# Split weights kept in DRAM and loaded again, small loads in program order, cache copies in parts: a hybrid attention and SSD layer on one core

## The chip, the cores and the metric

The kernel runs on 1 core of one Trainium2 chip. The metric is device time in microseconds (us). TensorE (PE), VectorE (DVE), ScalarE (ACT) and GpSimd (POOL) compute; SyncE (SP) issues all of the DMAs of this kernel.

## What is computed

One layer of a hybrid decoder on 2048 prompt tokens and 64 sample tokens, width 1024, all in float32:

```
h = rms_norm(x); proj = h @ w_in          # q k v z_a z_s xBC dt g
o_a = window attention (128, 16 heads, sinks, rope on a quarter of a head) * silu(z_a)
o_s = rms_norm(SSD scan of silu(conv(xBC)) * silu(z_s))
y   = x + (sigmoid(g_a) * (o_a @ w_attn_proj) + sigmoid(g_s) * (o_s @ w_ssd_proj)) @ w_out
```

It returns y of both groups, the last 128 keys and values (for the sample group: the caches, moved up by 8 rows, with the new rows behind), the conv rows and the SSM states.

## The kernel before, in words

The prompt is cut into four blocks (0 to 3) of 512 tokens. Three phases each run over the four blocks: T1 (attention's projections and the attention), S (the projections of the SSD branch, conv, and the scan in chunks of 128), and T2 (output projections). The sample tokens ride along in block 2 of T1 and block 0 of S.

A float32 product is made of three products of rounded parts: weights and activations are split into a high part and the rest (`SPLIT3`, L36). A weight tile has 256 columns of w_in by 1024 rows. `wload` (L161) loads it raw (1 MB, L157, pool `wraw` with 2 buffers); `split` (L149) then copies it on ACT to the high part (L150) and subtracts that on DVE (L151); both parts stand in `whl`, 2 MB, of which a phase has two buffers. So the tile after next can be filled only when PE has left a buffer. T1 has 10 tiles in a block, in the order za0, za1, k, v (with 32 more columns for dt), q0, q1, q2, q3, za2, za3; S has in each block 4 groups of 5: bc, x0, x1, z0, z1. Every block loads and splits the same weights again.

PE's projections are L171 (za tiles), L195 (k, v, q tiles, 96 matmuls each) and L184 (S and T2; a tile of S in blocks 1 to 3 has 48 matmuls of 512 columns). Attention units (L522 scores, L539 transposes, L551 products with the values) of one pair of heads run between the tiles that follow; each ends in a DMA of its result, `oa_d` (L563). At the end of a block `load_h` (L315) loads the next block's `hT` in 8 DMAs of 512 KB. In S the scan of group g (`ssd_group`) runs between the projections of group g+1; it ends in a sum of squares on PE (L907), whose row goes through DRAM three times: `ss_d` (L910), `sr` (L914, then the power on POOL), `rs_d` (L917).

`init3` (L227) loads small constants: conv rows, 16 sinks for the sample, `A_log`, `dt_bias`, and `Dcol` (L246: two loads of 64x16 single floats, every second float of D_skip). It is called when block 3 of T1 begins. The copy of the two caches to the output (L643) stands in the sample's attention, behind S.

What runs when on an engine is decided by a scheduler that simulates the program as it is built and may move an instruction ahead of others that it doesn't depend on. All DMAs go through SP's one queue in the order so made: a DMA that has to wait holds up those behind it.

Of the kernel before, what the change touches and what calls it, by code (L numbers as in the profile page):

```python
# [9 lines left out]
F32 = mybir.dt.float32  # L10
F32R = mybir.dt.float32r
# [17 lines left out]
OFF_X = 4608  # L29
# [49 lines left out]
def build(tc, nc, a, o, seq, phases=("T1", "S", "T2"), dbg=None):  # L79
# [66 lines left out]
    wraw_p = top.enter_context(tc.tile_pool(name="wraw", bufs=2))  # L146
    cur = {}

# [11 lines left out]

    def wload(parts):  # L161
        raw, hl = wtile(parts)
        split(hl[:, 0, :, :256], hl[:, 1, :, :256], raw)
        return raw, hl

    def proj_cm(ps, hl, c0, hT, first=True, last=True):
# [49 lines left out]
    def init2():  # L216
# [159 lines left out]
    def phase_t1():  # L376
        with ExitStack() as es:
# [32 lines left out]
            def za_tile(b, pair, hgp, hT, zs):  # L410
                raw, hl = wtile(za_parts(pair, hgp))
                r5 = raw.rearrange("p k (v h d) -> p k v h d", v=2, h=2)
                for hgl in range(2):
                    ov = [hl[:, i, :, hgl * P : hgl * P + P].rearrange("p k (v d) -> p k v d", v=2) for i in range(2)]
                    split(ov[0], ov[1], r5[:, :, :, hgl, :])
                for hgl in range(2):
# [191 lines left out]
    def phase_sa(oas):  # L608
        with ExitStack() as es:
# [108 lines left out]
    def phase_s():  # L718
        with ExitStack() as es:
# [75 lines left out]
            def proj_group(b, g, hT):  # L795
# [14 lines left out]
                for i in range(2):  # L810
                    c = 512 * g + 256 * i
                    _, hl = wload([(0, w_in[:, OFF_X + c : OFF_X + c + 256])])
                    st = sample_tile(smp)
                    for j in range(2):
                        pcs = prompt_pieces(proj_w(mmp, hl, j * P, hT, smp), st[:, j] if smp else None)
                        conv_tile(pcs, 4 * g + 2 * i + j, xT[:, 2 * i + j])
                    if smp:
                        SY.dma_start(xs_d[:, 4 * g + 2 * i : 4 * g + 2 * i + 2], st)
                for i in range(2):
                    c = 512 * g + 256 * i  # L820
                    _, hl = wload([(0, w_in[:, OFF_ZS + c : OFF_ZS + c + 256])])
                    st = sample_tile(smp)
# [506 lines left out]
```

## Time and profile before

| | before |
|---|---|
| median of 3 runs | 3202.14 us (3200.97 to 3202.41) |
| the profiled execution's own time | 3201.39 us |
| its span, first to last instruction | 3199.6 us |
| mean granted TensorE clock | 0.989 of full speed |
| PE busy | 3085.4 us (96%) |
| PE weight loads | 2649.2 us (83%) |
| DVE, ACT, POOL busy | 2081.5 (65%), 1419.9 (44%), 982.5 us (31%) |
| DMA | 448.88 MB, mean 140 GB/s, share of 16 engines 45.2% |

A busy share is of the whole span. T1 takes about the first 717 us, S until about 1944, T2 the rest. The waits of an engine are put down to what came last by the profile; the timeline gives for each stretch of like instructions its start and length, and in brackets how long the engine idled before it and for whom.

### The profile page before, as it was taken

To read this page: it belongs to the slowest core of one execution; us is meant where nothing else is said; L and a number is where in the kernel's file an instruction comes from. 1 tells how busy PE (TensorE), PEld (TensorE's weight loads), DVE (VectorE), ACT (ScalarE), POOL (GpSimd) and SP (SyncE) were. 2 spreads that over 40 slices of the span, in tenths; PEclk is the share of its full clock that TensorE was granted. 3 is DMA by queue.
4 is the path that set the end of the run, shared out by engine and by line. 5 is a ranking of instruction groups with operands and counts; after the bars stand their busy time and mean duration, and the time that the engine had idled before them with its cause. 6 is when DMAs were issued, how large, how long until landed. Compare 5 with 4: busy or idle time off the path is not lost.

```text
span 3199.6 us, 49248 instructions
## 1 busy us (share of the span) xinstructions
PE 3085.4 (96%) x19038; PEld 2649.2 (83%) x19038; DVE 2081.5 (65%) x3265; ACT 1419.9 (44%) x2786; POOL 982.5 (31%) x905
## 2 busy tenths in 40 slices
PE   6999999998999999999999998999999999999999
PEld 5978787877899877777777776787877799999888
DVE  3877868787777787888878886455555554334433
ACT  3544535455555555555656564333233333222321
POOL 1523232231445555555656664000121100000000
PEclk8999999999999999999999998999999999999999
DMA  6544425333433544444454444445655564345443
GB/s 215 157 141 117 141 76 180 108 107 103 126 121 119 172 130 124 154 148 131 129 167 147 129 141 128 139 131 154 205 181 143 155 206 132 99 132 175 137 107 103
DMA packets 472931, 448.88 MB, mean 140 GB/s; under 512 B 33824, under 2 KB 420664, under 8 KB 472648
## 3 DMA queue, kind: packets, MB, share of 16 engines
q1 hardware_dynamic: 472696, 445.73, 45.2%
q8 instruction: 150, 2.46, 0.3%
q14 instruction: 85, 0.70, 0.1%
HBM read 382.39 MB, written 65.35 MB: 140 GB/s over the span
## 4 chain that ended last, share of the span: by engine, by line
PE 73%; DVE 12%; DMA 5%; POOL 5%; issue 3%; ACT 2%; SPq 0%; POOLq 0%; DVEq 0%; ACTq 0%
PE mm L184 46%; PE mm L195 12%; PE mm L171 5%; DVE acc L760 3%; DVE whl L151 2%; POOL L L857 2%; DMA raw<-in_w_in_dram 2%; PE sc L522 1%; PE tr L551 1%; POOL ws L881 1%; DVE zs L897 1%; PE tr L539 1%; PE st L884 1%; DMA xt<-in_x_prompt_dram 1%; ACT whl L150 1%
## 5 line engine op out<-in xcount | busy, mean ns | idle before, releaser
L184 PE MATMUL mm<-hT,whl 128*128 128x512 f32 (+1 forms) x6720 | 1349.1, 357 | 10.4 <-DMA hT<-h_d 4.1
L184 PEld LDWEIGHTS mm<-hT,whl 128*128 128x128 f32 x6720 | 1119.5, 190 | 181.1 <-issue 12.6
L151 DVE TENSOR_TENSOR whl<-raw,whl 128x2048 fp32r<-128x2048 f32 (+1 forms) x232 | 524.6, 2265 | 280.4 <-ACT whl L150 273.0
L184 PE MATMUL mm<-ot,whl 128*128 128x512 f32 (+1 forms) x2880 | 569.1, 355 | 2.8 <-DVE whl L151 2.5
L184 PEld LDWEIGHTS mm<-ot,whl 128*128 128x128 f32 x2880 | 474.2, 188 | 74.9 <-issue 5.7
L150 ACT CAST whl<-raw 128x2048 fp32r<-128x2048 f32 (+1 forms) x232 | 412.7, 1786 | 263.3 <-PE mm L184 132.5
L195 PE MATMUL mm<-whl,hT 128*128 128x256 f32 (+1 forms) x2304 | 307.8, 289 | 23.7 <-DVE zs L421 17.2
L195 PEld LDWEIGHTS mm<-whl,hT 128*128 128x128 f32 x2304 | 290.7, 192 | 28.2 <-DVE zs L421 17.9
L760 DVE SCALAR_TENSOR_TENSOR acc<-cr,cwb,acc 128x512 f32<-128x512 f32 x288 | 284.5, 990 | 15.8 <-ACT acc L755 7.0
L857 POOL TENSOR_TENSOR L<-L,cbm 128x1024 f32<-128x1024 f32 x64 | 182.5, 2861 | 94.4 <-DVE cbm L846 92.8
L195 PE MATMUL mm<-whl,ot 128*128 128x256 f32 (+1 forms) x1632 | 203.9, 285 | 0.0
L195 PEld LDWEIGHTS mm<-whl,ot 128*128 128x128 f32 (+1 forms) x1632 | 197.6, 188 | 5.3 <-issue 4.9
L171 PE MATMUL mm<-hT,whl 128*128 128x512 f32 x768 | 194.3, 403 | 2.3 <-ACT hT L277 2.1
L855 ACT ACTIVATE L<-AB,acs 128x128 f32<-128x128 f32 x512 | 157.0, 389 | 38.6 <-PE py L878 29.0
L171 PEld LDWEIGHTS mm<-hT,whl 128*128 128x128 f32 x768 | 142.8, 192 | 33.8 <-ACT hT L277 2.5
L368 ACT ACTIVATE s<-s,ng 128x128 f32<-128x128 f32 x256 | 99.9, 393 | 94.4 <-DVE ng L362 84.2
L150 ACT CAST ot<-v 128x512 fp32r<-128x512 f32 x96 | 58.9, 620 | 162.1 <-DVE v L1195 86.9
L881 POOL TENSOR_TENSOR ws<-wx,ws 128x512 fp32r<-128x512 f32 x64 | 112.2, 1752 | 10.1 <-ACT ws L880 9.8
L374 POOL TENSOR_SCALAR s<-s,den 128x128 f32<-128x128 f32 x128 | 50.1, 403 | 202.7 <-DVE den L370 140.6
L826 ACT ACTIVATE th<-mm 128x512 f32<-128x512 f32 (+1 forms) x80 | 40.0, 509 | 160.8 <-PE mm L184 153.6
L764 ACT ACTIVATE th<-acc 128x512 f32<-128x512 f32 x96 | 60.5, 630 | 111.8 <-DVE acc L760 111.7
L1187 ACT ACTIVATE t<-mm 128x512 f32<-128x512 f32 (+1 forms) x76 | 37.6, 518 | 162.4 <-PE mm L184 141.9
(318 smaller groups left out, 3912.5 us busy)
## 6 DMA issues: line engine op xcount, KB each, us to landing
raw<-in_w_in_dram SPq DMA_DIRECT2D x120, 1024.0 KB
hT<-h_d SPq DMA_DIRECT2D x80, 512.0 KB
raw<-in_w_in_dram SPq DMA_DIRECT2D x64, 512.0 KB
AB<-ac_d SPq DMA_DIRECT2D x64, 512.0 KB
raw<-in_w_ssd_proj_dram SPq DMA_DIRECT2D x32, 1024.0 KB
v_d<-zs SPq DMA_DIRECT2D x16, 1024.0 KB
v<-v_d SPq DMA_DIRECT2D x64, 256.0 KB
raw<-in_w_attn_proj_dram SPq DMA_DIRECT2D x64, 256.0 KB
```

The costliest lines, as they stand in the source:

```text
L150: A.copy(hi, src)
L151: V.tensor_tensor(lo, src, hi.bitcast(F32), ALU.subtract)
L171: PE.matmul(ps, hl[:, x, k, c0 : c0 + P], ht[:, y, :], start=first and i == 0, stop=last and i == n - 1,)
L184: PE.matmul(ps, hl[:, x, k, c0 : c0 + P], ht[:, y, lo : lo + n], start=i == 0, stop=i == 3 * len(hT) - 1,)
L195: PE.matmul(ps, ht[:, x, tt * P : tt * P + m], hl[:, y, k, :n], start=i == 0, stop=i == 3 * len(hT) - 1,)
L368: A.activation(s[:, i, :width], s[:, i, :width], AF.Exp, bias=ng[:, i : i + 1], accum_out=den[:, i : i + 1])
L374: G.tensor_scalar(s[:, i, :width], s[:, i, :width], den[:, i : i + 1], 0.5, ALU.mult, ALU.mult)
L760: V.scalar_tensor_tensor(out=acc, in0=raw[:, k : k + TB], scalar=cwb[:, k, ct : ct + 1], in1=acc, op0=ALU.mult, op1=ALU.add)
L764: A.activation(th, acc, AF.Tanh)
L855: A.activation(L[:, h], AB[:, h], AF.Relu, scale=-1.0, bias=acs[:, hc.start + h : hc.start + h + 1])
L857: G.tensor_tensor(L, L, cbm[:, c].unsqueeze(1).to_broadcast([P, 8, P]), ALU.mult)
L881: G.tensor_tensor(ws[:, 1], wx, ws[:, 0].bitcast(F32), ALU.subtract)
```

## The change

Three edits; T2, and the arithmetic, are as before, and PE's instructions are the same in kind and number.

1. `store` writes the split tile `whl` (2 MB) to DRAM when a block has first made it: 10 tiles in T1's block 0 and 20 in S's block 0. `reload` loads such a tile (2 MB) straight to `whl` in blocks 1 and 3 of T1 (20 tiles; block 2 has the sample, which needs the raw tile, and loads and splits as before) and in blocks 1 to 3 of S (60 tiles). These 80 tiles have no raw load, no copy on ACT and no subtraction on DVE.
2. The small loads of `init3` are kept in program order by `late`: they can't be moved ahead of DMAs that stand before them in the program.
3. The copies of the caches, two DMAs of 960 KB, become 16 of 120 KB, a pair behind each second group of S, in program order too.

```diff
-    def wload(parts):
+    def wload(parts, key=None, keep=True):
+        if key in kept:
+            return None, reload(key)
         raw, hl = wtile(parts)
         split(hl[:, 0, :, :256], hl[:, 1, :, :256], raw)
+        if key is not None and keep:
+            store(key, hl)
         return raw, hl
+
+    def store(key, hl, w=256):
+        if key not in kept:
+            kept[key] = dt_("w_d" + "_".join(map(str, key)), [P, 2, KT, w]), w
+            SY.dma_start(kept[key][0], hl[:, :, :, :w].bitcast(F32))
+
+    def reload(key):
+        hl = cur["whl"].tile([P, 2, KT, cur["w"]], F32R, name="whl", tag="whl")
+        src, w = kept[key]
+        SY.dma_start(hl[:, :, :, :w].bitcast(F32), src)
+        return hl
...
+    def late(dst, src):
+        tc.keep_in_program_order(SY.dma_start(dst, src))
...
         for hl in range(2):
-            SY.dma_start(Dcol[64 * hl : 64 * hl + 64], dv[hl].partition_broadcast(64))
+            late(Dcol[64 * hl : 64 * hl + 64], dv[hl].partition_broadcast(64))
...
             def za_tile(b, pair, hgp, hT, zs):
+                key = ("za", pair, hgp)
+                if key in kept and b != sb:
+                    hl = reload(key)
+                else:
...
+                    store(key, hl)
...
-                raw, hl = wload([(0, w_in[:, OFF_K : OFF_K + 256])])
+                raw, hl = wload([(0, w_in[:, OFF_K : OFF_K + 256])], None if b == sb else ("k",))
...
-                SY.dma_start(ow[:, 0:120], a[f"cache_{nm}"][0].rearrange("b j h d -> b j (h d)")[:, 8:P])
...
-                _, hl = wload([(0, w_in[:, cb : cb + P]), (P, w_in[:, cc : cc + P])])
+                _, hl = wload([(0, w_in[:, cb : cb + P]), (P, w_in[:, cc : cc + P])], ("bc", g))
...
                     stats(b, g)
+                    for nm in ("k", "v"):
+                        for r in range((4 * b + g) * 8 // (4 * NB), (4 * b + g + 1) * 8 // (4 * NB)):
+                            late(o[f"{nm}_win_s"][r, 0:120], a[f"cache_{nm}"][0, r, 8:P].rearrange("j h d -> j (h d)"))
```

The other tiles of T1 and S get their keys in the same way. The order of the instructions follows from the scheduler, so it is shown at four places. Lines of the changed kernel are numbered otherwise: there L173 is `store`, L178 `reload`, L243 the loads of `late`; L300 is L282 of before, L308 is L290, L333 is L315, L588 is L563, L876, L886, L922, L934, L938 and L941 are L852, L862, L898, L910, L914 and L917. Names with numbers at their end are tensors in DRAM; 128x1024 of `hT` is 512 KB.

**The start, on SP** (T1's block 0, tiles k and v). Before:

```order
L240 DMA A_bc<-in_A_log_dram 128x32
L282 DMA h_d_1_61<-hT 128x1024
L243 DMA dtb_bc<-in_dt_bias_dram 128x32
L246 DMA Dcol<-in_D_skip_dram 64x16x1 x2
L290 DMA xt<-in_x_prompt_dram 128x1024
L282 DMA h_d_1_61<-hT 128x1024
L290 DMA xt<-in_x_prompt_dram 128x1024
L643 DMA out_dram<-in_cache_k_dram 8x2x15360
L282 DMA h_d_1_61<-hT 128x1024
L643 DMA out_dram<-in_cache_v_dram 8x2x15360
L157 DMA raw<-in_w_in_dram 128x8x256 x3
```

And now:

```order
L173 DMA w_dza_0_332<-whl 2048x1x256
L157 DMA raw<-in_w_in_dram 128x8x256
L300 DMA h_d_0_60<-hT 128x1024 x3
L173 DMA w_dza_1_398<-whl 2048x1x256
L157 DMA raw<-in_w_in_dram 128x8x256
L300 DMA h_d_0_60<-hT 128x1024
L599 DMA tab_2450<-in_rope_p_dram 128x4x80
L300 DMA h_d_1_61<-hT 128x1024 x2
L308 DMA xt<-in_x_prompt_dram 128x1024 x2
L300 DMA h_d_1_61<-hT 128x1024 x2
L173 DMA w_dk<-whl 2048x1x256
L157 DMA raw<-in_w_in_dram 128x8x256
```

The small loads of `init3` are gone from here, `Dcol` among them, and so are the cache copies; the stores of the tiles za0, za1, k and v stand between the others.

**The end of T1's block 0, on SP**, where the next block's `hT` is loaded. Before:

```order
L563 DMA oa_d_0_68<-zs 128x4x128
L157 DMA raw<-in_w_in_dram 128x8x256
L315 DMA hT<-h_d_0_62 128x1024 x4
L563 DMA oa_d_0_68<-zs 128x4x128
L315 DMA hT<-h_d_1_63 128x1024 x4
```

And now:

```order
L588 DMA oa_d_0_68<-zs 128x4x128
L178 DMA whl<-w_dza_1_398 128x16x256
L333 DMA hT<-h_d_0_62 128x1024 x4
L333 DMA hT<-h_d_1_63 128x1024 x3
L588 DMA oa_d_0_68<-zs 128x4x128
```

The reload of za1 for block 1 (`w_dza_1_398`) stands directly ahead of the 8 loads of `hT`; it writes to the buffer that PE's last tile of block 0 (za3) reads. **On PE** this is now the end of block 0 (L186 is L171 of before, L564 and L576 are L539 and L551), the last row being block 1's first tile:

```order
L186 MATMUL mm<-hT,whl 128x512 x2
L576 MATMUL tr<-PT,vT 64x512 x4
L564 MATMUL tr<-cst,s 128x128 x8
L576 MATMUL tr<-PT,vT 64x512 x4
L564 MATMUL tr<-cst,s 128x128 x8
L186 MATMUL mm<-hT,whl 128x512 x12
```

Between the last matmul of za3 and the first of block 1 there are two products with the values and two runs of transposes.

**T1's block 3, on SP**, from the results of block 2's last attention unit on. Before:

```order
L563 DMA oa_d_1_73<-zs 128x4x128
L446 DMA out_dram<-qr 128x256
L475 DMA out_dram<-vT 128x256
L157 DMA raw<-in_w_in_dram 128x8x256
L563 DMA oa_d_1_73<-zs 128x4x128
L473 DMA dt_d_115<-dtt 128x128
L157 DMA raw<-in_w_in_dram 128x8x128 x6
```

And now:

```order
L588 DMA oa_d_1_73<-zs 128x4x128
L243 DMA rows_6516<-in_conv_w_dram 96x128
L243 DMA rows_6516<-in_conv_b_dram 24x128
L243 DMA rows_6516<-in_ssd_norm_w_dram 16x128
L243 DMA sinkS<-in_sinks_dram 8x1 x16
L243 DMA A_bc<-in_A_log_dram 128x32
L243 DMA dtb_bc<-in_dt_bias_dram 128x32
L243 DMA Dcol<-in_D_skip_dram 64x16x1 x2
L498 DMA dt_d_115<-dtt 128x128
L500 DMA out_dram<-vT 128x256
L178 DMA whl<-w_dq_924 128x16x256
L178 DMA whl<-w_dq_1536 128x16x256
```

The small loads now stand here; the reload of q1 (`w_dq_924`) is behind them.

**The end of a group in S, on SP.** Before (a raw bc tile is two loads of 128 columns):

```order
L898 DMA v_d_1_81<-zs 128x4x512
L157 DMA raw<-in_w_in_dram 128x8x128 x2
L157 DMA raw<-in_w_in_dram 128x8x256
L910 DMA ss_d_1_101<-sm 1x512
L914 DMA sr<-ss_d_1_101 128x4
L917 DMA rs_d_1_121<-sr 128x4
L157 DMA raw<-in_w_in_dram 128x8x256 x2
```

And now, with a pair of cache copies:

```order
L922 DMA v_d_1_85<-zs 128x4x512
L886 DMA EB<-ac_d_94 64x4x128
L178 DMA whl<-w_dz_1_10873 128x4096
L934 DMA ss_d_1_105<-sm 1x512
L938 DMA sr<-ss_d_1_105 128x4
L941 DMA rs_d_1_125<-sr 128x4
L243 DMA out_dram<-in_cache_k_dram 16x1920
L243 DMA out_dram<-in_cache_v_dram 16x1920
L178 DMA whl<-w_dbc_11240 128x4096
```

The raw loads of bc and x0 stood ahead of `ss_d` before; now the reload of the next group's bc stands behind `rs_d` and the copies. The same place **on PE** now (L931 is L907 of before, L199 is L184, L862 to L890 are the first steps of the next scan, ahead of the next bc tile):

```order
L199 MATMUL mm<-hT,whl 128x512 x59
L931 MATMUL st<-thl,onesr 32x512
L199 MATMUL mm<-hT,whl 128x512 x5
L931 MATMUL st<-thl,onesr 32x512
L199 MATMUL mm<-hT,whl 128x512 x25
L862 MATMUL tr<-cst,BT 128x128
L199 MATMUL mm<-hT,whl 128x512 x48
L862 MATMUL tr<-cst,BT 128x128 x3
L868 MATMUL tr<-CT,BT 128x128 x4
L890 MATMUL po<-CT,H_8427 128x128 x4
L199 MATMUL mm<-hT,whl 128x512 x19
```

Behind the second L931 there are 25 and 48 matmuls of the tiles z0 and z1 and then 8 short instructions before the first matmul of the next bc tile.

## Rows read from the trace of the kernel before

**Rows 1.** Windows by stage: us, busy of each engine (instructions), PE clock, DMA share, GB/s.

```profile
0.00:200.00 200.00, 165.85 (x1056) 145.35 (x1057) 120.67 (x223) 86.37 (x185) 58.40 (x77) 0.95 0.60 191
200.00:707.00 507.00, 497.07 (x3564) 427.46 (x3564) 389.09 (x838) 242.12 (x718) 155.67 (x215) 0.99 0.37 113
717.00:1066.00 349.00, 333.40 (x2480) 312.36 (x2478) 249.22 (x419) 189.62 (x429) 144.65 (x131) 0.97 0.38 119
1066.00:1944.00 878.00, 850.32 (x4522) 689.00 (x4522) 712.96 (x808) 511.06 (x896) 513.15 (x401) 1.00 0.45 143
```

**Rows 2.** PE's waits, whole span: engine, line, releaser: us, times, longest us.

```profile
PE mm L195 <- DVE zs L421: 17.2, 2, 16.1
...
PE py L878 <- DVE xT L894: 10.2, 9, 1.3
...
PE po L866 <- DVE H L891: 7.7, 13, 1.2
```

**Rows 3.** Timeline at the start, all engines: start us, us, engine, line, operation.

```profile
40.22 0.33 SPq L243 DMA_DIRECT2D dtb_bc<-in_dt_bias_dram  x1
...
40.59 1.44 SPq L246 DMA_DIRECT2D Dcol<-in_D_skip_dram  x2
...
52.29 5.80 SPq L290 DMA_DIRECT2D xt<-in_x_prompt_dram  x1
...
63.94 1.06 ACT L251 ACTIVATE junk<-xt 128x1024 bf16<-128x1024 f32 x1 [20.95 <-DMA xt<-in_x_prompt_dram]
...
66.34 1.01 PE L195 MATMUL mm<-whl,hT 128*128 128x256 f32 x3 [16.10 <-DVE zs L421]
```

**Rows 4.** Windows, columns as in group 1: two stretches of the start, then T1's end.

```profile
42.00:61.00 19.00, 7.13 (x54) 6.34 (x52) 2.33 (x3) 0.23 (x1) 0.00 (x0) 0.85 0.06 7
55.30:72.40 17.10, 6.06 (x28) 6.06 (x29) 6.11 (x6) 5.86 (x9) 1.46 (x4) 0.50 0.62 244
714.00:721.00 7.00, 4.32 (x19) 4.32 (x20) 6.84 (x17) 2.22 (x4) 1.28 (x1) 0.51 1.04 384
```

**Rows 5.** The page's costliest groups: the split of the weights on VectorE and ScalarE.

```profile
L151 DVE TENSOR_TENSOR whl<-raw,whl 128x2048 fp32r<-128x2048 f32 (+1 forms) x232 | 524.6, 2265 | 280.4 <-ACT whl L150 273.0
...
L150 ACT CAST whl<-raw 128x2048 fp32r<-128x2048 f32 (+1 forms) x232 | 412.7, 1786 | 263.3 <-PE mm L184 132.5
```

**Rows 6.** SP's queue, timeline at the end of T1's block 0.

```profile
168.91 2.42 SPq L315 DMA_DIRECT2D hT<-h_d  x4
```

**Rows 7.** PE's timeline in T1's block 3: parts of tiles v and q0.

```profile
600.79 4.76 PE L195 MATMUL mm<-whl,hT 128*128 128x288 f32 x34
...
605.48 1.94 PE L551 MATMUL tr<-PT,vT 128*64 128x512 f32 x8
...
607.76 5.44 PE L195 MATMUL mm<-whl,hT 128*128 128x288 f32 x39
...
620.28 4.75 PE L195 MATMUL mm<-whl,hT 128*128 128x256 f32 x38
```

**Rows 8.** SP's queue, timeline in S, block 1: two group ends.

```profile
1198.12 0.25 SPq L910 DMA_DIRECT2D ss_d<-sm  x1
1200.76 0.35 SPq L914 DMA_DIRECT2D sr<-ss_d  x1
1203.88 0.33 SPq L917 DMA_DIRECT2D rs_d<-sr  x1
...
1266.14 0.39 SPq L910 DMA_DIRECT2D ss_d<-sm  x1
1270.79 0.35 SPq L914 DMA_DIRECT2D sr<-ss_d  x1
1275.67 0.33 SPq L917 DMA_DIRECT2D rs_d<-sr  x1
```

**Rows 9.** PE's timeline in S, block 1, at the second of those group ends.

```profile
1263.89 0.40 PE L907 MATMUL st<-thl,onesr 128*32 128x512 f32 x1
1264.12 16.49 PE L184 MATMUL mm<-hT,whl 128*128 128x512 f32 x72
```

More of the change, by code (lines that the diff above doesn't have):

```diff
@@ L146, in build @@
     wraw_p = top.enter_context(tc.tile_pool(name="wraw", bufs=2))
-    cur = {}
+    cur, kept = {}, {}
     def split(hi, lo, src, **kw):
@@ L225, in init2 @@
         V.tensor_scalar(wrow[:, 0], wrow[:, 0], 0.125, None, ALU.mult)
+    def late(dst, src):
+        tc.keep_in_program_order(SY.dma_start(dst, src))
     def init3(xp, trp):
         rows = xp.tile([P, 2, P], F32, name="rows3", tag="xt")
-        SY.dma_start(rows[:96, 0], a["conv_w"][0].rearrange("k (c p) -> (k c) p", p=P))
-        SY.dma_start(rows[96:120, 0], a["conv_b"][0].rearrange("(c p) -> c p", p=P))
-        SY.dma_start(rows[:16, 1], a["ssd_norm_w"][0].rearrange("(c p) -> c p", p=P))
+        late(rows[:96, 0], a["conv_w"][0].rearrange("k (c p) -> (k c) p", p=P))
+        late(rows[96:120, 0], a["conv_b"][0].rearrange("(c p) -> c p", p=P))
+        late(rows[:16, 1], a["ssd_norm_w"][0].rearrange("(c p) -> c p", p=P))
         ips = trp.tile([P, 256], F32, name="tr", tag="tr")
@@ L237, in init3 @@
         for h in range(NH):
-            SY.dma_start(sinkS[8 * h : 8 * h + 8], a["sinks"][0][h : h + 1].partition_broadcast(8))
+            late(sinkS[8 * h : 8 * h + 8], a["sinks"][0][h : h + 1].partition_broadcast(8))
         V.tensor_scalar(nsinkS, sinkS, -1.0, None, ALU.mult)
-        SY.dma_start(A_bc, a["A_log"][0].partition_broadcast(P))
+        late(A_bc, a["A_log"][0].partition_broadcast(P))
         A.activation(A_bc, A_bc, AF.Exp)
         V.tensor_scalar(A_bc, A_bc, -1.0, None, ALU.mult)
-        SY.dma_start(dtb_bc, a["dt_bias"][0].partition_broadcast(P))
+        late(dtb_bc, a["dt_bias"][0].partition_broadcast(P))
         dv = a["D_skip"][0].rearrange("(c l) -> l c", l=2)
         for hl in range(2):
-            SY.dma_start(Dcol[64 * hl : 64 * hl + 64], dv[hl].partition_broadcast(64))
+            late(Dcol[64 * hl : 64 * hl + 64], dv[hl].partition_broadcast(64))
     def norm_x(xt, jp, nwb, n=P):
@@ L410, in za_tile @@
             def za_tile(b, pair, hgp, hT, zs):
[L411 to L415, printed above, removed]
+                key = ("za", pair, hgp)
+                if key in kept and b != sb:
+                    hl = reload(key)
+                else:
+                    raw, hl = wtile(za_parts(pair, hgp))
+                    r5 = raw.rearrange("p k (v h d) -> p k v h d", v=2, h=2)
+                    for hgl in range(2):
+                        ov = [hl[:, i, :, hgl * P : hgl * P + P].rearrange("p k (v d) -> p k v d", v=2) for i in range(2)]
+                        split(ov[0], ov[1], r5[:, :, :, hgl, :])
+                    store(key, hl)
                 for hgl in range(2):
@@ L462, in v_tile @@
                     SY.dma_start(raw_dt, w_in[:, OFF_DT : OFF_DT + 32].rearrange("(k p) c -> p k c", p=P))
-                raw, hl = wload([(0, w_in[:, OFF_V : OFF_V + 256])])
-                split(hl[:, 0, :, 256:288], hl[:, 1, :, 256:288], raw_dt)
+                raw, hl = wload([(0, w_in[:, OFF_V : OFF_V + 256])], None if b == sb else ("v",), keep=False)
+                if raw is not None:
+                    split(hl[:, 0, :, 256:288], hl[:, 1, :, 256:288], raw_dt)
+                    store(("v",), hl, 288)
                 if b > 0:
@@ L484, in q_tile @@
             def q_tile(b, kv, hT, tab):
-                raw, hl = wload([(0, w_in[:, kv * 256 : kv * 256 + 256])])
+                raw, hl = wload([(0, w_in[:, kv * 256 : kv * 256 + 256])], None if b == sb else ("q", kv))
                 out = []
@@ L811, in proj_group @@
                     c = 512 * g + 256 * i
-                    _, hl = wload([(0, w_in[:, OFF_X + c : OFF_X + c + 256])])
+                    _, hl = wload([(0, w_in[:, OFF_X + c : OFF_X + c + 256])], ("x", g, i))
                     st = sample_tile(smp)
@@ L820, in proj_group @@
                     c = 512 * g + 256 * i
-                    _, hl = wload([(0, w_in[:, OFF_ZS + c : OFF_ZS + c + 256])])
+                    _, hl = wload([(0, w_in[:, OFF_ZS + c : OFF_ZS + c + 256])], ("z", g, i))
                     st = sample_tile(smp)
```

## The prediction

> **What bounds the kernel now.** I read the windows by stage first, since a busy share over the whole span mixes three phases. PE is the engine that is always nearly full: it is idle for 34.2 of the first 200 us, for 9.9 us up to 707 us, for 15.6 us in S's first block and for 27.7 us in the other three blocks of S (length of the stretch less PE's busy time) [rows 1]. DVE is next, at 713.0 of 878 us in S's blocks 1 to 3. So the copies and subtractions that the change takes away, long as they are, sit on engines that have room, and the change is worth what it does to PE's idle time and PE's clock. PE's own waits come second: the largest single one is 16.1 us at a place where DVE makes `zs` [rows 2]; the others are many and about 1 us each, on DVE's `xT` and `H`. Third, the timeline of the start shows where the 16.1 us come from [rows 3]: the two `Dcol` loads are issued at 40.59, the issue of the `xt` load behind them takes 5.80 us, and in 42 to 61 us the DMA engines carry 7 GB/s at a share of 0.06 [rows 4]. Those loads are 2048 pieces of 4 bytes; they block the queue for about 20 us. ACT waits 20.95 us for `xt`, and PE's wait ends when ACT and DVE go on. Afterwards the granted clock is 0.50 until 72.4 us [rows 4], which is the level of 1.2 GHz.
>
> All sums are against the profiled execution, 3201.39 us; the median of the three runs is 0.75 us above that, so what holds for one holds for the other. A difference under 0.2%, 6.4 us, can't be told from none here.
>
> **The start.** The `Dcol` loads leave, and with them the sinks' loads that held up DVE. PE's wait of 17.2 us [rows 2] goes, and the 6.1 us of work at half clock behind it (66.34 to 72.4) [rows 3, 4] takes 3.0 less: -20. What is late next: two stores of 2 MB now stand ahead of the v tile's raw load, and two more follow. At the 384 GB/s that the queue reached at the end of T1 [rows 4], 2 MB is 5.5 us. K's raw load is then some 5.5 us later and v's 11, and both still come while PE is on the tiles before (za1 and k, over 11 us each), so I cost the stores at nothing here; if that cover is gone, see the third rival.
>
> **The end of T1's block 0.** The reload of za1 must wait until PE has left za3, and the 8 `hT` loads are behind it. Before, four of them were issued at 168.91, with PE still on za3 [rows 6]. Now hT's first 512 KB come 5.5 us (2 MB) and 1.4 us later, plus a completion of 1.5 to 3 us (the round trip of a load of 2 KB is 2.6 us from issue to issue) [rows 8], so 8.4 to 10 us after za3. PE has two products of 1.94 us [rows 7] and the transposes between, some 6 us. The stall is 3 to 4 us; a pause of this kind has cost some time at half clock as well. I take +7, from +3 to +10.
>
> **Block 3 of T1.** `Dcol` is still loaded, only later, and the reload of q1 is queued behind it. Counted from the start of v: unit 3's result is at about +12, since its products stand in the middle of v; 21 small loads at 0.33 us [rows 3] put `Dcol` at +19; it drains until +39, by the 20 us of the start; 2 MB more land at +45. PE wants q1 after v (96 matmuls at 139 ns [rows 7]: 13.4 us), q0 (96 at 125 ns: 12.0 us) and transposes: about +30. That is a stall of 15 us, with 3 us of half clock as at the start: +18. Before, nothing of the kind stood there. So the largest stall is moved, not removed.
>
> **S, block 0.** 20 stores of 2 MB in 349 us add 120 GB/s to the 119 there [rows 1]; a store follows the split and its buffer is read by PE for longer than it takes. +3 for queueing, bounds 0 and +10.
>
> **S, blocks 1 to 3.** 60 tiles lose 1.8 us of ACT and 2.27 us of DVE [rows 5], some 245 us of the two engines, none of it on PE's path as such. What it can give back is PE's idle time, 27.7 us [rows 1], which is mostly the short waits for DVE (10.2 us for `xT`, 7.7 us for `H`) [rows 2]. DVE loses 11.4 us in a group of 73 us, so I let half of it go: -14 (nothing at the one end, -25 at the other). Against that stand the reloads. A buffer is free when PE leaves a tile and wanted one tile later, 48 matmuls of 229 ns, 11.0 us [rows 9]; 2 MB need 5.5 us at the 384 GB/s and at most some 10 with a slow round trip, so a reload that is issued at once comes in time. The bc tile of the next group isn't: its reload is behind `ss_d`, `sr`, `rs_d` and two copies. From PE's second L907 it was 2.2 us to `ss_d` [rows 8, 9]; the two steps behind took 2.6 and 3.1 us at the one group end and 4.7 and 4.9 us at the other [rows 8]; with 1.1 us for the copies' issue the reload is issued at +9.0 to +12.9 us and lands between +15 and +22. PE wants it after 73 matmuls, 16.7 us, and 2 us of short work: +18.7. The middle, about 18.5, is just in time. I take half a microsecond late on average over 12 groups: +6, bounds 0 and +40. Sum for these blocks: -8.
>
> The Trainium skill has a rule for this (DMA: Bandwidth & Descriptors, "Anatomy of one DMA": a transfer costs about 2.0 us plus its bytes over 436 GB/s, fitted for DMAs that GpSimd issues). It would give an estimate of 6.8 us for a reload, with the chain as above +15.8 to +19.7; by it the bc tile is late in the worst case only, these blocks give -14, and the total is 6 us lower. I stay with the rows, whose best rate is 384 GB/s.
>
> **The rest.** T1's blocks 1 and 3 lose 20 splits, and their idle time is small (9.9 us in 507) [rows 1]; the cache copies leave the busy start. -5, bounds -10 and 0. T2 is unchanged. **Sum:** -20 + 7 + 18 + 3 - 8 - 5 = -5, so about 3196 us. Its own range is 3180 to 3212, by the bounds above.
>
> **Rivals.**
> 1. *The reloads come late in S, and the kernel is slower.* The place is the bc tile at the 12 group ends; it decides once load and chain exceed 18.7 us. With the slow steps (+12.9) and a 2 MB load of 9 us it is 3.2 us late: 12 x 3.2 = 38, and the -14 shrinks too, since the tiles behind z1 are held by the same queue; 3196 - 6 + 38 = 3228, up to 3240. For it: the queue carries twice the bytes, and the steps of 4.7 us were measured with 2 MB of raw loads in flight. Against: there, three raw loads were ahead of `ss_d`, and now it is one reload, issued 6 us earlier. A sentence of the Trainium skill speaks for it (DMA: Bandwidth & Descriptors, "Latency and other measured facts": access to HBM takes 0.2 us on average and 2 us at high load); the steps of 2.6 and 4.7 us agree with a latency that grows under load. Chance 0.24.
> 2. *`Dcol` in block 3 doesn't reach PE* (it drains faster when nothing else is asked for, or q1's order differs in time): without the +18, 3178. Against it: the 19 us of nearly empty DMA engines [rows 4] had no other traffic in them. Chance 0.17.
> 3. *The stall at the start stays*: stores of 2 MB ahead of the raw loads and of `xt` take the place of `Dcol`. 8 MB at 384 GB/s are 22 us of queue, and if half of that falls on PE, +12, with its clock: 3211. Against it: each load has over 11 us of PE's work as cover. Chance 0.12.
>
> **How the numbers follow.** The forecast has 0.47. Faster by over 0.2% is below 3195.7, slower above 3208.5. The forecast lies at the first bound; of its 0.47 I give 0.25 to faster, 0.17 to the same and 0.05 to slower; the first rival is slower (0.22) or, if only just late, the same (0.02), the second is faster (0.17), the third slower (0.08) or the same (0.04). So faster 0.42, the same 0.23, slower 0.35. The range of 8 in 10 goes from 3168 (the second rival with a little more of S's waits gone) to 3232 (most of the first).
>
> **What would show it.** Right: no wait of 16 us of PE near 50 us; a wait of PE at the start of q1 in block 3 of 10 us or more with the DMA engines nearly empty ahead of it; a few us of waiting for `hT` at the end of block 0; in S's blocks 1 to 3, PE's waits for `xT` and `H` about halved, and a wait for the bc reload of under 1 us per group. Wrong: waits of PE on reloads of several us at each group end (first rival), no wait at q1 (second), a wait near 50 us for k or v (third).

## The result, and the profile after

The changed kernel took 3184.4 us (median of 4 runs, 3183.07 to 3188.17) beside 3202.27 us (4 runs, 3200.97 to 3208.05): a ratio of 0.9943, 95% interval 0.9925 to 0.9960. It is faster, by 0.4 to 0.75%. The profiled execution has a span of 3182.0 us at a mean clock of 0.990, 17.6 us less than before. DMA moved 596.45 MB instead of 448.88.

The 17.6 us are the small remainder of larger amounts of both signs. The table gives the time at which PE begins or ends certain tiles, found by counting the matmuls of its projection lines in the trace (48 or 96 a tile). The lead is after less before; a step is what the lead changed by since the row above.

| mark | before | after | lead | step |
|---|---|---|---|---|
| T1 block 0: q1 begins | 102.5 | 83.6 | -18.9 | -18.9 |
| block 0: za3 ends | 177.6 | 157.8 | -19.8 | -0.9 |
| block 1: za1 ends | 213.9 | 200.3 | -13.6 | +6.2 |
| block 1: q0 begins | 255.4 | 236.6 | -18.8 | -5.2 |
| block 2: first tile begins | 349.7 | 329.6 | -20.1 | -1.3 |
| block 3: q0 ends | 631.8 | 610.3 | -21.6 | -1.5 |
| block 3: q1 begins | 631.7 | 628.3 | -3.4 | +18.2 |
| block 3: za3 ends | 707.2 | 708.8 | +1.5 | +4.9 |
| S: first tile begins | 717.4 | 713.0 | -4.5 | -6.0 |
| S: block 1 begins | 1068.0 | 1066.7 | -1.3 | +3.2 |
| S: last tile ends | 1943.9 | 1929.0 | -14.9 | -13.6 |
| end of the span | 3199.6 | 3182.0 | -17.6 | -2.7 |

The order of PE's attention units differs between the two kernels, so a mark can stand ahead of work that the other kernel has already done. At q1 of block 0 and at block 2's first tile both have done the same (the count in brackets behind PE's busy time is of its matmuls), before and after:

```profile
102.50:349.70 247.20, 240.62 (x1642) 210.78 (x1641) 195.41 (x426) 131.36 (x368) 86.34 (x115) 0.99 0.49 148
```

```profile
83.63:329.60 245.97, 239.30 (x1643) 208.89 (x1642) 181.98 (x419) 114.59 (x353) 83.65 (x118) 0.99 0.75 240
```

Between them the lead grows by 1.3 us, and PE idles for as long as before (6.7 us for 6.6). In the step of +6.2 at za1's end PE does 190 matmuls where it had done 159 (from za3's end on, both with 96 of the projections): attention work that had its place before za3's end or behind za1's. Of the -5.2 behind it 3.6 us are a wait for `dtt` that PE no longer has.

**The start.** PE's timeline after, where 16.10 us of idle time stood [rows 3]:

```profile
43.71 16.51 PE L210 MATMUL mm<-whl,hT 128*128 128x256 f32 x133
```

and ACT's, in the same place:

```profile
43.91 0.60 ACT L443 ACTIVATE th<-mm 128x512 f32<-128x512 f32 x1 [2.34 <-PE mm L186]
...
47.34 1.91 ACT L150 CAST whl<-raw 128x2048 fp32r<-128x2048 f32 x1 [2.54 <-DMA raw<-in_w_in_dram]
...
52.88 1.06 ACT L269 ACTIVATE junk<-xt 128x1024 bf16<-128x1024 f32 x1 [2.66 <-DMA xt<-in_x_prompt_dram]
```

PE goes through k and v without a pause. ACT's tanh comes ahead of its work on `xt`, and that waits 2.66 us for its load instead of 20.95.

**Block 3 of T1.** SP's queue after:

```profile
593.11 5.38 SPq L243 DMA_DIRECT2D sinkS<-in_sinks_dram  x16
...
599.41 1.37 SPq L243 DMA_DIRECT2D Dcol<-in_D_skip_dram  x2
600.88 3.20 SPq L498 DMA_DIRECT2D dt_d<-dtt  x1
604.18 0.74 SPq L500 DMA_DIRECT2D out_dram<-vT  x1
605.01 17.25 SPq L178 DMA_DIRECT2D whl<-w_dq  x2
```

PE's timeline there:

```profile
611.96 0.63 PE L521 MATMUL tr<-cst,qr 128*128 128x128 f32 x4 [1.26 <-DVE qr L369]
628.29 8.31 PE L210 MATMUL mm<-whl,hT 128*128 128x256 f32 x49 [15.70 <-DMA whl<-w_dq]
```

and the windows at that place (columns as in [rows 1]):

```profile
616.30:633.40 17.10, 5.11 (x24) 5.14 (x25) 0.20 (x1) 0.00 (x0) 0.00 (x0) 0.50 0.79 257
```

`Dcol` is issued at 599.41, 18.1 us after v began (k ended at 581.4). The issues of the two reloads behind it end only 17.25 us after the first began; q1's is out by 606.1, but from 604 to 616 us the DMA engines are at a share of 0.05 and carry nothing that counts (0 GB/s). PE waits 15.70 us for q1's reload, and the clock is granted at 0.50, the level of 1.2 GHz, until 633.4.

**The end of block 0.** SP and PE, after:

```profile
158.59 0.78 SPq L178 DMA_DIRECT2D whl<-w_dza  x1
...
160.03 5.53 SPq L333 DMA_DIRECT2D hT<-h_d  x7
...
164.95 2.98 PE L576 MATMUL tr<-PT,vT 128*64 128x512 f32 x8 [3.02 <-DVE PT L566]
...
169.97 3.06 PE L186 MATMUL mm<-hT,whl 128*128 128x512 f32 x12 [0.43 <-DMA hT<-h_d]
```

hT is issued 2.2 us after za3's end at 157.8 and PE starts on it at 169.97. In between PE has only attention units, with waits of 1.13 and 3.02 us for `PT`, DVE's copy of their transposed weights. The last wait is the one for hT (0.43 us): without the waits for `PT`, PE would have waited for hT instead, and block 1 could not have begun much earlier.

**PE's waits over the whole span**, after [rows 2]:

```profile
PE mm L210 <- DMA whl<-w_dq: 15.7, 1, 15.7
...
PE py L902 <- DVE xT L918: 5.1, 5, 1.3
PE po L890 <- DVE H L915: 5.0, 2, 2.6
```

The waits for `xT` are half of the 10.2 us of before, those for `H` 5.0 instead of 7.7. The windows after, S's block 0 and blocks 1 to 3:

```profile
717.00:1066.00 349.00, 329.76 (x2450) 307.41 (x2449) 242.93 (x418) 186.39 (x428) 143.25 (x130) 0.98 0.72 244
...
1066.70:1929.00 862.30, 849.04 (x4509) 688.10 (x4507) 577.14 (x745) 404.51 (x830) 439.79 (x401) 1.00 0.63 218
```

In blocks 1 to 3 PE is idle for 13.3 us (862.30 less 849.04), where it had been 27.7; DVE has 577 us of work instead of 711 in the same stretch of before. In block 0 the stores raise the traffic from 119 to 244 GB/s. The splits that are left, on the page after [rows 5]:

```profile
L151 DVE TENSOR_TENSOR whl<-raw,whl 128x2048 fp32r<-128x2048 f32 (+1 forms) x144 | 319.4, 2221 | 253.9 <-ACT whl L150 248.9
...
L150 ACT CAST whl<-raw 128x2048 fp32r<-128x2048 f32 (+1 forms) x144 | 259.6, 1810 | 239.7 <-PE mm L199 128.2
```

205 us of DVE and 153 us of ACT are gone, and 17.6 us of the span.

**The end of a group in S**, block 1, after, on SP and on PE:

```profile
1251.95 0.32 SPq L178 DMA_DIRECT2D whl<-w_dz  x1
1259.84 0.24 SPq L934 DMA_DIRECT2D ss_d<-sm  x1
1260.97 0.33 SPq L938 DMA_DIRECT2D sr<-ss_d  x1
1264.00 0.32 SPq L941 DMA_DIRECT2D rs_d<-sr  x1
...
1265.69 0.53 SPq L178 DMA_DIRECT2D whl<-w_dbc  x1
```

```profile
1257.22 0.40 PE L931 MATMUL st<-thl,onesr 128*32 128x512 f32 x1
...
1276.17 4.13 PE L199 MATMUL mm<-hT,whl 128*128 128x512 f32 x17
```

From the second L931 to the first matmul of the next bc tile it is 18.95 us; its reload is issued at +8.5 us, and PE doesn't wait for it. The trace has ten group ends whose reload stands behind `rs_d` in this way: it is issued at +7.2 to +13.6 us (median 9.6), and PE begins the tile 9.5 to 12.9 us after the issue, at none of them waiting for the reload. All waits of PE for reloads in blocks 1 to 3 come to 0.7 us.

### The profile page after: what moved, and what is told of

Its sections match the earlier page's. It is cut to its first block, busy times and chain, and to the rows that moved or that the text cites. A ratio compares the mean times of both kernels' runs of the same rounds, so it can differ in the third digit from the quotient of the medians.

```text
span 3182.0 us, 49035 instructions
## 1 busy us (share of the span) xinstructions
PE 3085.6 (97%) x19038; PEld 2647.9 (83%) x19038; DVE 1905.2 (60%) x3175; ACT 1279.3 (40%) x2696; POOL 900.8 (28%) x905
## 2 busy tenths in 40 slices
DMA packets 437073, 596.45 MB, mean 187 GB/s; under 512 B 34224, under 2 KB 373960, under 8 KB 426200
## 4 chain that ended last, share of the span: by engine, by line
PE 76%; DVE 9%; DMA 6%; POOL 4%; issue 3%; ACT 2%; SPq 1%; DVEq 0%; ACTq 0%; POOLq 0%
PE mm L199 50%; PE mm L210 11%; PE mm L186 5%; DVE acc L784 2%; PE tr L576 2%; DMA hT<-h_d 2%; PE sc L547 1%; PE py L902 1%; POOL ws L905 1%; POOL L L881 1%; PE st L908 1%; PE po L890 1%; PE tr L564 1%; DMA whl<-w_dq 1%; DMA h_d<-hst 1%
## 5 line engine op out<-in xcount | busy, mean ns | idle before, releaser
L199 PE MATMUL mm<-hT,whl 128*128 128x512 f32 (+1 forms) x6720 | 1343.6, 356 | 11.5 <-DMA hT<-h_d 6.9
L199 PEld LDWEIGHTS mm<-hT,whl 128*128 128x128 f32 x6720 | 1116.9, 189 | 182.9 <-issue 12.5
L199 PE MATMUL mm<-ot,whl 128*128 128x512 f32 (+1 forms) x2880 | 571.7, 356 | 2.2 <-ACT ot L150 2.2
L199 PEld LDWEIGHTS mm<-ot,whl 128*128 128x128 f32 x2880 | 476.1, 189 | 74.7 <-issue 5.7
L151 DVE TENSOR_TENSOR whl<-raw,whl 128x2048 fp32r<-128x2048 f32 (+1 forms) x144 | 319.4, 2221 | 253.9 <-ACT whl L150 248.9
L150 ACT CAST whl<-raw 128x2048 fp32r<-128x2048 f32 (+1 forms) x144 | 259.6, 1810 | 239.7 <-PE mm L199 128.2
L784 DVE SCALAR_TENSOR_TENSOR acc<-cr,cwb,acc 128x512 f32<-128x512 f32 x288 | 274.2, 953 | 27.2 <-ACT acc L779 24.8
L881 POOL TENSOR_TENSOR L<-L,cbm 128x1024 f32<-128x1024 f32 x64 | 162.2, 2545 | 143.8 <-DVE cbm L870 136.9
L186 PE MATMUL mm<-hT,whl 128*128 128x512 f32 x768 | 192.9, 401 | 3.4 <-ACT hT L295 2.3
L186 PEld LDWEIGHTS mm<-hT,whl 128*128 128x128 f32 x768 | 141.7, 190 | 35.4 <-ACT hT L295 2.7
L851 DVE SCALAR_TENSOR_TENSOR zs<-th,mm 128x512 f32<-128x512 f32 (+1 forms) x80 | 45.7, 578 | 150.0 <-ACT th L850 149.4
L905 POOL TENSOR_TENSOR ws<-wx,ws 128x512 fp32r<-128x512 f32 x64 | 105.8, 1653 | 5.1 <-ACT ws L904 4.9
```

The source lines that it names most:

```text
L150: A.copy(hi, src)
L151: V.tensor_tensor(lo, src, hi.bitcast(F32), ALU.subtract)
L186: PE.matmul(ps, hl[:, x, k, c0 : c0 + P], ht[:, y, :], start=first and i == 0, stop=last and i == n - 1,)
L199: PE.matmul(ps, hl[:, x, k, c0 : c0 + P], ht[:, y, lo : lo + n], start=i == 0, stop=i == 3 * len(hT) - 1,)
L784: V.scalar_tensor_tensor(out=acc, in0=raw[:, k : k + TB], scalar=cwb[:, k, ct : ct + 1], in1=acc, op0=ALU.mult, op1=ALU.add)
L881: G.tensor_tensor(L, L, cbm[:, c].unsqueeze(1).to_broadcast([P, 8, P]), ALU.mult)
```

## The experiments

Each ratio is against runs of the kernel before on the same chip in the same session; the medians of before were 3202.3 to 3205.5 in them, so ratios are compared, and medians only within a few us. Marks are those of the table above.

**1. Reloads without the new order.** The small loads may be moved again, and the cache copies are as before.

```diff
     def late(dst, src):
-        tc.keep_in_program_order(SY.dma_start(dst, src))
+        SY.dma_start(dst, src)
```

> Stores and reloads as in the changed kernel, but the small loads and the cache copies free to be moved, as before. Theory A (the moved loads took the stall from the start, about -19 us, and put it at q1 of block 3, about +18; the reloads are worth about -14 in S's blocks 1 to 3): PE's stall of some 16 us near 50 us is back, no stall at q1, so the two cancel and the time is that of the changed kernel within 6 us, 3184 (3178 to 3190). In the order hT stands ahead of za1's reload, which should take some 5 us off the end of block 0: 3180 is likeliest. Theory B (the whole gain is the moved loads; the reloads give nothing): 3200.

Measured: 3185.17 us, ratio 0.9943 (0.9926 to 0.9959). PE's longest wait, from its waits over the whole span:

```profile
PE mm L210 <- ACT whl L150: 19.3, 1, 19.3
```

SP's queue in that run:

```profile
57.99 0.97 SPq L243 DMA_DIRECT2D Dcol<-in_D_skip_dram  x1
59.01 1.34 SPq L668 DMA_DIRECT2D out_dram<-in_cache_k_dram  x1
60.40 0.68 SPq L668 DMA_DIRECT2D out_dram<-in_cache_v_dram  x1
61.20 5.44 SPq L173 DMA_DIRECT2D w_dk<-whl  x1
66.69 21.11 SPq L157 DMA_DIRECT2D raw<-in_w_in_dram  x1
```

The stall is back at the start, at 78.5 us instead of 50 and 19.3 us long: the two `Dcol` loads were moved to 54 and 58 us, and the raw load behind them takes 21 us to issue. It isn't `Dcol`'s alone: the cache copies (1.9 MB) and the store of k (2 MB) stand between, and from 80 to 82 us, with PE idle, the DMA engines are at a share of 0.91. There is none at q1. With hT ahead of za1's reload the step at the end of block 0 is 1.2 us (lead +7.6 at za3's end, +8.8 at za1's) where it was 6.2, with 182 matmuls in it for 190. So the reloads alone are worth what the change is worth, though the stall of the start stays; theory B falls.

**2. The new order without reloads.** No tile is stored.

```diff
-        if key is not None and keep:
-            store(key, hl)
...
-                    store(key, hl)
...
-                    store(("v",), hl, 288)
```

> The small loads in program order and the cache copies in parts, no stores and no reloads. Theory A: no stall at the start (-19), a stall at block 3 behind Dcol of 10 to 18 us (a raw load of 1 MB and the split behind it instead of 2 MB): 3195 to 3202, about 3199. Theory B (the moved loads are the gain): 3184.

Measured: 3184.15 us, ratio 0.9939 (0.9925 to 0.9954). That is the number of theory B, and a miss for mine: the start is 22.1 us shorter, and no stall comes up at block 3, where the lead at q1 is still -22.8. SP's queue and the windows there:

```profile
598.88 0.39 SPq L157 DMA_DIRECT2D raw<-in_w_in_dram  x1
...
611.64 1.40 SPq L241 DMA_DIRECT2D Dcol<-in_D_skip_dram  x2
```

```profile
611.00:632.00 21.00, 21.00 (x182) 21.00 (x181) 15.64 (x28) 8.63 (x14) 13.86 (x12) 1.00 0.06 4
```

The DMA engines are as empty behind `Dcol` as before (share 0.06, 4 GB/s), and PE doesn't idle there. A raw load waits for a raw buffer and not for PE's, so q1's stands ahead of `Dcol` in the queue and has landed. So both halves of the change are worth 18 to 20 us alone, and together no more: the order frees the start, and the reload of q1 puts the same 20 us of queue on PE again.

**3. Reloads in T1 alone.** The keys of S's tiles are left out.

```diff
-                _, hl = wload([(0, w_in[:, cb : cb + P]), (P, w_in[:, cc : cc + P])], ("bc", g))
+                _, hl = wload([(0, w_in[:, cb : cb + P]), (P, w_in[:, cc : cc + P])])
```

> Stores and reloads in T1 alone, S loads and splits as before; small loads in order. Theory A: the changed kernel without S's share (+3 in block 0, -14 in blocks 1 to 3, -3 behind): 3184 + 14 = 3198. Theory B: 3184.

Measured: 3193.39 us, ratio 0.9968 (0.9958 to 0.9979). The lead is -2.8 at q1 of block 3, as in the changed kernel, and -6.0 at S's block 1 and at S's end: nothing comes of S's blocks 1 to 3. Nearer to theory A, 5 us under its number.

**4. Reloads in S alone**, with the new order; T1 loads and splits.

> Stores and reloads in S alone, T1 loads and splits as before, small loads in order. By marks in the traces so far: the run with the order alone ends S's first stretch 10 us early, S's block 0 with stores costs 5 us more than without, blocks 1 to 3 with reloads 12 us less. Theory A (S's reloads pay, T1's don't): about 7 us under the run with the order alone, 3177. Theory B (reloads give nothing anywhere): 3184.

Measured: 3176.13 us, ratio 0.9906 (0.9886 to 0.9926), as theory A had it. The steps by marks: -23.0 at q1 of block 3, then 13 us lost until S's first tile, +2.0 in S's block 0, -15.4 in blocks 1 to 3.

**5. The changed kernel with D_skip as one row.**

```diff
-        dv = a["D_skip"][0].rearrange("(c l) -> l c", l=2)
+        late(Drow, a["D_skip"][0].partition_broadcast(P))
         for hl in range(2):
-            late(Dcol[64 * hl : 64 * hl + 64], dv[hl].partition_broadcast(64))
+            V.tensor_copy(Dcol[64 * hl : 64 * hl + 64], Drow[64 * hl : 64 * hl + 64].rearrange("p (c l) -> p l c", l=2)[:, hl])
```

> The changed kernel, with D_skip loaded as one row of 32 floats to every partition (128 pieces of 128 bytes instead of 2048 of 4 bytes) and two copies on VectorE to Dcol. Theory A (the stall at q1 is the Dcol load's 20 us ahead of q1's reload in the queue): PE's wait of 15.7 us at q1 goes, with the half clock behind it: 3184 - 18 = 3166. Rival C (the stall is the other 21 small loads, or the time at which the last attention unit lets the queue go on): a wait of 8 us or more stays at q1, 3176 to 3184.

Measured: 3168.52 us, ratio 0.9886 (0.9871 to 0.9901). PE has no wait at q1; the lead there is -18.2 instead of -3.4. SP's queue in that run:

```profile
600.49 0.42 SPq L244 DMA_DIRECT2D Drow<-in_D_skip_dram  x1
601.01 0.38 SPq L499 DMA_DIRECT2D dt_d<-dtt  x1
...
601.97 9.96 SPq L179 DMA_DIRECT2D whl<-w_dq  x2
```

The 21 other small loads stand where they stood, so rival C falls: the stall is the form of this one load.

**6. S's reloads with the row.** As run 4, with the edit of run 5.

> As the run before, with D_skip loaded as one row of 32 floats. With raw loads q1 stands ahead of Dcol in the queue and PE has no stall there, but the run with the order alone loses 12 us between q2 of block 3 and S's first tile, with a PE wait of 8.3 us. If Dcol's 20 us in the queue are behind that, too: 12 us under the run before, 3165. If that loss is the order of the attention units: no change against the run before, 3177.

Measured: 3169.90 us, ratio 0.9891 (0.9871 to 0.9912): 6 us under run 4, between the two cases. PE's waits between 600 and 760 us in that run:

```profile
PE tr L563 <- DVE s L391: 11.2, 3, 8.3
```

The wait of 8.3 us stands there as in run 4, so it isn't `Dcol`; that the order of the last attention units makes it is likely and wasn't tried by itself. Of the 13 us that run 4 loses here some 5 were the queue; 8 are left. Beside run 5 it also says that T1's stores and reloads together are worth nothing that can be measured: 3169.9 without them, 3168.5 with them.

**7. Without the two reloads of block 1's za tiles**, with the row.

```diff
-                if key in kept and b != sb:
+                if key in kept and b != sb and (b, pair, hgp) not in ((1, 0, 0), (1, 0, 1)):
```

> As the changed kernel with D_skip as one row, but za0 and za1 of block 1 are loaded raw and split, so that no reload waits for PE ahead of hT. Theory A (hT and the attention units at the end of block 0 are held up by the reload of za1, worth 5 to 6 us): 3168 less 5 = 3163. Rival (the loss there comes with any order of the units): 3168.

Measured: 3168.86 us, ratio 0.9882 (0.9860 to 0.9904), no different from run 5. The lead at block 2's first tile is 6 us larger (-24.8 for -18.8), but PE has done 24 matmuls fewer by then (2050 for 2074). At block 2's k tile both have done 2305, and run 7 is 1.1 us ahead (369.4 for 370.5 us). The changed kernel, with the same instructions as run 5 in T1 so far, comes to this place at 369.1, so such a difference says nothing. PE does idle less between za3 and block 1 (2.3 us for 5.7), but theory A's 5 us aren't there at block 2, nor at the end.

**8. The kernel before with the row, and nothing else.**

> The kernel before with nothing changed but the load of D_skip (one row of 32 floats and two copies on VectorE). Theory A (the stall at the start is the 2048 small pieces and nothing else): PE's wait of 16 us near 50 us goes, 3202 less 19 to 22 = about 3182. Rival D (ACT's xt work ahead of the tanh of k's tile stalls PE whatever is ahead in the queue, or the other small loads do): 3195 to 3202.

Measured: 3189.85 us, ratio 0.9950 (0.9930 to 0.9970). PE's timeline there:

```profile
43.61 11.84 PE L196 MATMUL mm<-whl,hT 128*128 128x256 f32 x97 [0.29 <-DVE zs L422]
57.41 3.33 PE L196 MATMUL mm<-whl,hT 128*128 128x288 f32 x23 [1.96 <-DVE whl L152]
```

The wait of 16 us is gone, with the other small loads and ACT's order as they were: the small pieces were the stall, and rival D falls. The step at the start is -15.6 and not -19 to -22, because two waits of 2.0 and 1.8 us come up for v's split and k's norm; the time is 8 us over theory A's number. The sinks' loads stand where they stood, so they had no part in the stall. What runs 5 and 8 change together is the size of the pieces and their number. The form of one load is thus alone worth nearly as much as the whole change.

**9. and 10. Which engine S's gain hangs on.** Run 6 with a spare operation behind each reload, a subtraction of 128x2048 on DVE (run 9) or a copy on ACT (run 10):

```diff
         SY.dma_start(hl[:, :, :, :w].bitcast(F32), src)
+        raw = wraw_p.tile([P, KT, 256], F32, name="raw", tag="raw")
+        V.tensor_tensor(raw.bitcast(F32R), hl[:, 0].bitcast(F32), hl[:, 1].bitcast(F32), ALU.subtract)
```

> S's reloads with the D_skip row, as in the run of 3170, and behind each reload one subtraction of 128x2048 on VectorE into the unused raw tile, as long as the one that the reload had saved (2.3 us, 60 of them). Theory A (S's gain in blocks 1 to 3 is VectorE's freed time, which PE's short waits for xT and H hang on): those blocks take 12 to 18 us longer again, 3183 (3178 to 3188), with PE's waits on xT back at about 9 us. Rival E (the gain is ScalarE's freed time, or the simpler path of the weights): 3170.

> The same with a copy of 128x2048 on ScalarE (1.9 us, 60 of them) in place of the subtraction. Theory A: no change, 3170 (3166 to 3174). Rival E: 3180 or more.

Measured: 3204.39 us (ratio 0.9994, 0.9983 to 1.0005) with DVE's, 3173.50 us (0.9909, 0.9894 to 0.9923) with ACT's. ACT's 60 copies cost nothing in S: blocks 1 to 3 took 858.9 us with them (run 10, first row) and 858.1 without (run 6, second row):

```profile
1056.80:1915.70 858.90, 846.80 (x4509) 685.91 (x4508) 563.82 (x745) 509.29 (x889) 427.39 (x401) 1.00 0.62 221
```

```profile
1052.90:1911.00 858.10, 846.05 (x4509) 685.51 (x4508) 577.57 (x745) 405.09 (x830) 440.10 (x401) 1.00 0.62 219
```

Rival E falls. DVE's cost twice what was expected, and its waits in that run (blocks 1 to 3) say why it is no clean test:

```profile
DVE raw L181 <- DMA whl<-w_dbc: 20.4, 9, 8.0
...
DVE raw L181 <- DMA whl<-w_dx: 14.0, 4, 5.6
```

DVE stood still for loads, which the splits before hadn't made it do.

**11. The subtraction without a load to wait for.** Run 6 with one subtraction per tile on what DVE has just made itself:

```diff
+            def burn(src):
+                raw = wraw_p.tile([P, KT, 256], F32, name="raw", tag="raw")
+                x = src.unsqueeze(1).to_broadcast([P, 4, TB])
+                V.tensor_tensor(raw.rearrange("p (a k) c -> p a (k c)", a=4), x, x, ALU.subtract)
```

> S's reloads with the D_skip row (3170), and in S's blocks 1 to 3, once a tile, a subtraction of 128x2048 on VectorE whose operand is VectorE's own last output of the tile, so that it waits for no load (60 of them, 2.3 us each). The run with the subtraction behind each reload also made VectorE wait 43 us for loads. Theory A (VectorE's time alone is what S's gain hangs on): blocks 1 to 3 take 12 to 18 us more, 3183 (3178 to 3190), PE's waits for xT and H back at about 17 us. Rival F (only VectorE's waits for the loads did harm): 3170.

Measured: 3201.68 us, ratio 0.9989 (0.9980 to 0.9998). The windows of blocks 1 to 3, then PE's waits in them:

```profile
1057.00:1943.20 886.20, 854.62 (x4509) 689.89 (x4507) 713.79 (x804) 405.24 (x830) 491.69 (x401) 0.99 0.60 213
```

```profile
PE po L900 <- DVE H L925: 18.1, 14, 2.6
PE st L918 <- POOL ws L915: 10.1, 8, 1.7
```

DVE has 713.8 us of work again, as before (711.3 in the same stretch), with no wait for a load, and these blocks take 28 us more than in run 6: 19.5 us more of PE's idle time, with waits on `H` of 18.1 us where run 6 has 5.0, and 8.6 us more of busy time for the same matmuls. Rival F falls, and theory A's number is missed as well. The cost is twice the 12 to 18 us expected, and more than the splits had cost, so where in its order DVE works matters as well as how long; the order of PE differs between the two runs, too, and the two weren't separated. POOL goes with DVE: its 401 instructions of these blocks, the same in each run, took 513 us before, 440 in run 6, 492 here and 427 in run 10, and PE waits for its `ws` for 10.1 us here and 2.8 in run 6. How much of DVE's effect on PE comes by way of POOL wasn't separated either.

**12. T1's reloads in block 3 alone**, with the row.

> D_skip as one row, reloads in S and in block 3 of T1 alone; blocks 1 and 2 of T1 load and split. If T1's reloads cost at the end of block 0 (5 us) and pay in block 3, where the S-only run has a PE wait of 8.3 us: 3170 less 5 to 8, 3163. If T1's share is nothing but the order of its units: 3168 to 3171, as the other versions with the row.

Measured: 3175.56 us, ratio 0.9903 (0.9887 to 0.9920), 6 us over run 6. Both cases expected fall. In T1's blocks 0 and 1, where the stores stand and nothing is reloaded, the lead falls behind: -13.2 at q0 of block 1 where run 6, without stores, has -22.5. That the stores themselves do it is likely and wasn't tried by itself. But by S's first tile both are at -16 (-15.9 and -16.1), so block 3's reloads have won that back, and the difference of the two profiled executions is made behind it, in S and T2, whose code is the same in both. It has no cause that I could show; run 12's profiled execution is 5 us above its median, run 6's 3 us under.

The fastest versions are runs 5, 6 and 7, 1.1% under the kernel before and 0.5% under the changed one; their intervals overlap almost wholly.

## Why the prediction was right, and where its terms were not

The forecast was faster, 3196 us; it came to 3184.4, inside its own range (3180 to 3212). The two large terms, the stall that leaves the start and the stall that comes up at q1, were right in place, cause and size. But all terms together were to give 5 us and gave 17.6. The forecast lay at the bound between faster and the same, with a chance of 0.42 for faster, so the direction was in part luck: what made the gain clear are terms that I had too small.

- *The start, -20:* measured -18.9. The stall went; run 8 shows the cause alone. Two errors cancel in it: the five runs with T1's stores and the loads in order have a lead of -17.9 to -19.2 at q1, the six without stores -21.6 to -23.3. So the stores, which I costed at nothing, cost 3 to 4 us. V's split did get its load in time (it waited 2.54 us, while PE had k's tile), but in q0 PE waits 2.3 us for POOL's `kd`, which it doesn't in run 2; whether the stores' traffic or the order makes that is open.
- *The end of block 0, +7:* PE idled for 4.6 us, the last of it for `hT`, and did 3.4 us of work at half clock behind: some 6.3 us, so the term held. The +6.2 of the table agrees by chance, since other work stands in that step. What I left out are waits that went: 2.9 us for `qT` and `qr` at this place and 3.6 us for `dtt` at q0, so that with the same work done, at block 2's first tile, nothing of the 7 is left. The cause is not as sure as the size: without the reload ahead of hT (run 7) PE idles for 2.3 us there, and hardly anything of that reaches block 2. (The 2.6 us that I took for a load's round trip is the step from a store to the load behind it.)
- *Block 3, +18:* measured +18.2, a wait of 15.70 us and the half clock behind it. What I took for a fixed cost of the late loads is one of the pair with the reload: in run 2 the same loads cost nothing.
- *S's block 0, +3:* measured +3.2 by its own marks, +2.1 from q1 of block 3, where the order of T1's last units doesn't enter.
- *S's blocks 1 to 3, -8:* measured -13.6. The gain of 14 on the short waits was right in size; the 6 us for late bc reloads was the step that failed. I put the reload's issue at +9.0 to +12.9 us, from first steps of 2.6 and 4.7 us between `ss_d` and `sr` and second ones of 3.1 and 4.9; at seven of the ten group ends the first was 1.1 to 1.2 us, at all ten the second 2.9 to 3.1, so that the issue was at +9.6 in the middle, and PE's waits for reloads were 0.7 us in all. The load itself was within my 5.5 to 10 us: from 1267 to 1273 us the DMA engines carried 374 GB/s, 2.2 MB, so the reload that was issued at 1265.69 had landed some 7.3 us later (an estimate from that window). The Trainium skill's formula (DMA: Bandwidth & Descriptors, "Anatomy of one DMA"), by which a reload was estimated at 6.8 us and these blocks were to give the full 14, came nearer than I did.
- *The rest, -5:* too small. With the end of block 0 it was to be +2, and came to -2.7 from q1 of block 0 to q0 of block 3, so T1's waits that went are worth more than I gave them. T2, whose order is the same, adds -2.7 us, no more than executions of one kernel differ by.

The rivals: the first, late reloads, fell with the 0.7 us; the second, `Dcol` not reaching PE, with the 15.70; the third with the start. That ACT's time is worth nothing in S is shown by run 10. That DVE's is what S could use was in the forecast and is borne out by run 11, but twice over, so the 13.6 us aren't accounted for by DVE's time alone.

## What to carry to other kernels

Before moving a load that blocks a queue, ask what form it has: 2048 pieces of 4 bytes cost about 20 us of queue at the places where they were tried, and 128 pieces of 128 bytes with two small copies make no stall (runs 5 and 8). A load straight into the buffer that PE reads has lost the slack that a raw buffer ahead of it had, so anything slow in front of it in an in-order queue falls on PE at once (run 2 beside the changed kernel). And work taken off a busy engine is worth what the bound engine waits for it, in S's blocks 1 to 3 some 14 us of PE for 134 us of DVE, and nothing for 105 us of ACT. A mark in a timeline is a fair measure only where both kernels have done the same work: 24 matmuls left for later looked like 6 us of gain in run 7.

## What the runs showed of the hardware

- Two loads of 64x16 single floats leave the DMA engines at a share of 0.06 and 4 to 7 GB/s for about 20 us, at the start of the kernel before and in block 3 of run 2; their pieces go at an even 107 a us (1496 in the 14 us from 44 us on before, 1417 in the 13.2 us from 614.8 on in run 2). DMA issues behind them took up to 13 us there, and 21 us at 58 us in run 1, where other traffic stood between. The first of these places was known from the trace of before; that the pause comes along, and goes with the form of the load, was new.
- The step from the store of 2 KB to the load behind it took 1.1 to 1.2 us at seven of ten group ends, where it had taken 2.6 and 4.7 [rows 8]; at the one shown nothing had been issued for the 7.9 us before (1251.95 to 1259.84).
- PE's pauses go on costing behind them: after the 15.70 us at q1 the granted clock stayed at 0.50 for another 5.1 us of matmuls (628.29 to 633.4), and 3.4 us at 0.50 followed the 3.02 us at the end of block 0.
- POOL's products of 128x1024 (`L`) took 2985 ns each in S's blocks 1 to 3 before and 2530 in the changed kernel, 2951 in run 11 and 2550 in run 9, 2524 in run 10 (POOL's spans are rough in the profile). They are longer beside the splits and beside run 11's subtractions, not beside copies on ACT, and in run 9 as many subtractions at other places didn't lengthen them.
